# Pacing the projection products in groups of 12 and 24 in place of 5 and 8

## The chip, the core and the metric

One NeuronCore of a Trainium2 chip (trn2). The metric is device time in microseconds (us) of the whole program, which is launched once. Names of engines, as the profile gives them: PE is TensorE's matmul, PEld its weight load, DVE VectorE, ACT ScalarE, POOL GpSimd, SP the engine that issues all DMAs of this kernel. Every engine works off its own queue in a fixed order that was written down when the kernel was built; it waits where an instruction's input is not there yet, and everything behind that instruction on the same engine waits with it.

## What is computed

Two sequences of 1024 tokens (width 1024) go through the same two layers. Cut to what matters:

```python
def encoder_layer(x, c, p):
    shift, scale, gate = split(silu(c) @ w_ada + b_ada)
    h = rms_norm(x, g_pre) * (1 + scale) + shift
    proj = h @ w_in                              # the input projection
    o_a = latent_attention(...)                  # mixer a
    o_b = rwkv7(...)                             # mixer b, one scan per direction
    o_c = mamba2_ssd(...)                        # mixer c
    o_d = gated_deltanet(...)                    # mixer d, one scan per direction
    return x + gate * rms_norm(concat(o_a, o_b, o_c, o_d) @ w_out, g_post)   # the output projection
```

A pair (sequence, layer) is called a unit; there are four, run in the order (0,0), (1,0), (0,1), (1,1).

## The kernel before, in words

**Two kinds of work share TensorE.** The *bulk* is the two projections. Each fp32 operand is split into a high and a low part, and three products (high x high, high x low, low x high) stand for one fp32 product. `in_tile` makes a tile of 128 projected columns for 512 tokens: 8 slices of the contraction, three products of 128x512 each, 24 in all. Its weights come as two pairs (`halves`, high and low part of four slices), so one loaded pair feeds 12 products. `out_tiles` makes 256 output columns for 512 tokens; there a loaded pair feeds 24 products of 128x256. The whole program has 6144 products of the first kind and 3072 of the second. All of them are recorded at one line, L472, and write the tile `pj`.

The *mixers* are the rest: four heads' groups a, b, c, d with many small products, most of them 64x64, in chains that go from PE to DVE or ACT and back. Their lines that the text names: L1211, L1223, L1236, L1193 are the delta rule's scan (d); L921, L931, L944, L947, L878, L579, L891, L902 rwkv's scan (b), and L838 what prepares it; L1571 to L1573 and L1584 the attention (a); L244 the conditioning. `d` and `c` run beside each other, then `b` and `a`.

**What sets the order.** A scheduler fixes each engine's order at build time. It runs through an estimate of the program's time and takes, whenever an engine is free, the ready instruction of the highest priority. The priorities of a unit's bulk are spread over those of the mixers of the unit before (`behind`, `ahead`), so that projections of the next unit and of the last one lie between the mixers' instructions. So that the scheduler doesn't take all ready bulk at once, `paced` puts it in groups:

```python
    def paced(self, n, *mm):
        m = self.nc.tensor.matmul(*mm[:3], **mm[3]).ins
        if self.gate is not None:
            self.tc.add_manual_dep(m, self.gate[0], SYNC, reason="pace")
        if self.run == 0:
            t = self.nc.gpsimd.memset(self.token, 0.0).ins
            self.tc.add_manual_dep(t, m.name, SYNC, reason="pace")
            self.next = t.name
        self.run += 1
        if self.run == n:
            self.gate, self.run = (self.next,), 0
```

After the first product of a group, POOL sets a one-element tile, the *token* (L476). The products of the next group wait for that token. These are real semaphores: they hold on the chip as well as in the scheduler's estimate. POOL's other work is some 460 small instructions of the mixers, such as the edge memsets of rwkv's loads (L739, L741), the powers in norms (L156) and masks (L1353). The group size is `TK` for `in_tile` and `TO` for `out_tiles`. Counts of groups run on from one tile to the next.

Of the kernel before, what the change touches and what calls it, by code (L numbers as in the profile page):

```python
# [22 lines left out]
MIX = 1800  # L23
EA = 60
EB = 60
TK = 5
TO = 8
ED = 90
SB = 3
WB = 6  # L30
# [76 lines left out]
class Body:  # L107
# [204 lines left out]
    def in_tile(self, l, name, hf, hh, hl, Pd):  # L312
# [4 lines left out]
        for k in range(8):  # L317
            if k % 4 == 0:
                w2 = self.halves(("in", l, ci, k // 4), lambda: self.A["w_in"][l, ci][:, k * 128:k * 128 + 512]).rearrange("p u (k c) -> p u k c", k=4)
            for i, (a, b) in enumerate(((0, hh), (0, hl), (1, hh))):  # L320
                self.paced(TK, ps[0:M], w2[:, a, k % 4, 0:M], b[:, k, :], dict(start=(k == 0 and i == 0), stop=(k == 7 and i == 2)))
        st = self.t(pj, [128, 512], tag="st", bufs=SB)
# [26 lines left out]
    def out_tiles(self, l, ch, hh, hl, kqs, at=lambda kq: kq):  # L349
# [3 lines left out]
        for n, kq in enumerate(kqs):  # L353
            w2 = self.halves(("out", l, ch, kq), lambda: self.A["w_out"][l, ch, kq // 2][:, (kq % 2) * 512:(kq % 2) * 512 + 512]).rearrange("p u (k c) -> p u k c", k=2)
            for i in range(4):
                ps = pss[i // 2][:, i % 2]
                c = slice(i * 128, (i + 1) * 128)
                for k in range(2):
                    a, b = hh[:, at(kq) * 2 + k, c], hl[:, at(kq) * 2 + k, c]
                    first, last = n == 0 and k == 0 and i % 2 == 0, n == len(kqs) - 1 and k == 1  # L360
                    for m, (u, x) in enumerate(((a, 0), (a, 1), (b, 0))):
                        self.paced(TO, ps, u, w2[:, x, k], dict(start=first and m == 0, stop=last and m == 2, skip_group_check=True))
        return pss
# [1378 lines left out]
```

## Time and profile before

| | |
|---|---|
| median of 3 runs (lowest to highest) | 4653.71 us (4644.23 to 4672.16) |
| the profiled execution's own time | 4653.13 us |
| span from its first to its last instruction | 4651.1 us |
| PE / PEld / DVE / ACT / POOL busy | 90% / 68% / 65% / 39% / 8% of the span |
| mean granted TensorE clock | 0.895 of 2.4 GHz |

The span is 2.0 us shorter than the execution's own time, which is 0.6 us from the median. PE's busy time counts a product until its modelled end, and a product begins before the one ahead of it has ended, so two products of 0.4 us each can follow each other at 0.23 us. Rows of the trace say how long one instruction took, and in brackets how long its engine sat idle before it and what ended that.

### The profile page before, as it was taken

How to read it: one execution, taken by the hardware profiler on the slowest of the kernel's cores; microseconds unless marked ns; L12 is line 12 of the kernel's file. 1: busy time of each engine (PE TensorE's matmuls, PEld its weight loads, DVE VectorE, ACT ScalarE, POOL GpSimd, SP SyncE). 2: the span in 40 equal slices, each digit the busy share in tenths (PEclk: the TensorE clock that was granted, in tenths of full speed). 3: DMA queues.
4: the chain of work that ended last, by engine and by line, in shares of the span. 5: the costliest groups of instructions: out<-in, count | busy, mean ns of one | idle time of the engine just before them, and what ended most of it. 6: DMA issues, size and time to landing. Idle time of an engine off the chain costs nothing.

```text
span 4651.1 us, 98709 instructions
## 1 busy us (share of the span) xinstructions
PE 4177.0 (90%) x38484; PEld 3160.9 (68%) x38484; DVE 3012.1 (65%) x6237; ACT 1818.2 (39%) x4054; POOL 385.0 (8%) x2073
## 2 busy tenths in 40 slices
PE   6888998999998987989988999889897999989997
PEld 2667666667677766745767767767675776767776
DVE  2359587466559597476537959756633886865755
ACT  2433334362422433453434243335333324434433
POOL 0011001000011100000001100100001110000001
PEclk8889987989999987989989999888798999979888
DMA  5787664542676666573557767556355767665535
GB/s 205 282 268 250 236 198 152 190 145 91 203 221 228 207 190 203 151 218 134 199 194 241 256 230 215 177 182 179 123 173 183 227 225 225 209 226 151 173 114 173
DMA packets 518089, 912.85 MB, mean 196 GB/s; under 512 B 152312, under 2 KB 268536, under 8 KB 514040
## 3 DMA queue, kind: packets, MB, share of 16 engines
q1 hardware_dynamic: 517624, 906.54, 60.3%
q8 instruction: 305, 5.00, 0.4%
q14 instruction: 160, 1.31, 0.1%
HBM read 622.85 MB, written 283.43 MB: 195 GB/s over the span
## 4 chain that ended last, share of the span: by engine, by line
PE 43%; DMA 15%; DVE 13%; ACT 3%; issue 3%; SPq 1%; POOL 1%; DVEq 0%; POOLq 0%; ACTq 0%
PE pj L472 20%; PE b L838 2%; PE b L1584 1%; DVE iA L536 1%; DVE G L556 1%; SPq L145 1%; DMA G<-P 1%; PE b L1540 1%; PE b L1571 1%; PE pj L244 1%; DMA UV<-vd 1%; PE b L571 1%; DMA st<-yd 1%; DVE iT L543 1%; DMA P<-st 1%
## 5 line engine op out<-in xcount | busy, mean ns | idle before, releaser
L472 PE MATMUL pj<-hh,w 128*128 128x512 f32 (+1 forms) x4096 | 1428.5, 420 | 54.6 <-POOL token L476 27.1
L472 PEld LDWEIGHTS pj<-hh,w 128*128 128x128 f32 (+1 forms) x4096 | 785.4, 195 | 260.8 <-POOL token L476 39.8
L472 PE MATMUL pj<-hl,w 128*128 128x512 f32 (+1 forms) x2048 | 859.0, 420 | 29.8 <-POOL token L476 29.7
L472 PEld LDWEIGHTS pj<-hl,w 128*128 128x128 f32 (+1 forms) x2048 | 400.4, 195 | 130.5 <-POOL token L476 38.4
L476 POOL MEMSET token<- 1x1 f32 x1613 | 142.9, 89 | 3246.8 <-PE pj L472 3238.5
L472 PE MATMUL pj<-w,hh 128*128 128x256 f32 x1536 | 334.1, 309 | 10.2 <-ACT st L386 7.5
L472 PEld LDWEIGHTS pj<-w,hh 128*128 128x128 f32 x1536 | 263.0, 205 | 32.0 <-issue 15.5
L472 PE MATMUL pj<-w,hl 128*128 128x256 f32 x960 | 271.2, 310 | 0.0
L328 ACT COPY st<-pj 128x512 f32<-128x512 f32 (+1 forms) x192 | 112.0, 583 | 366.1 <-PE pj L472 319.4
L1575 ACT ACTIVATE pT<-b 128x512 f32<-128x512 f32 x256 | 150.2, 599 | 223.3 <-PE b L1573 219.0
L652 DVE SCALAR_TENSOR_TENSOR cva<-cvi,cw,cva 128x1024 f32<-128x1024 f32 x144 | 183.6, 1279 | 60.7 <-ACT cva L648 47.1
L1541 DVE TENSOR_REDUCE mx<-b 128x1 f32<-128x512 f32 x256 | 169.8, 685 | 57.2 <-PE b L1540 55.7
L472 PEld LDWEIGHTS pj<-w,hl 128*128 128x128 f32 x960 | 186.1, 205 | 12.9 <-issue 5.4
L342 ACT CAST w<-w 128x512 fp32r<-128x512 f32 x160 | 98.9, 619 | 244.5 <-DMA w<-w_in 163.4
L343 DVE TENSOR_TENSOR w<-w,w 128x512 fp32r<-128x512 f32 x160 | 113.2, 708 | 108.2 <-ACT w L342 102.2
L1219 ACT ACTIVATE SE<-SC,el 64x64 f32<-64x64 f32 x480 | 140.3, 338 | 80.5 <-DVE SC L1230 41.2
L1584 PEld LDWEIGHTS b<-VO,pT 128*64 128x64 f32 x4096 | 144.0, 146 | 36.6 <-issue 30.0
L938 DVE TENSOR_TENSOR ZS<-us,SE 64x128 f32<-64x128 f32 x240 | 69.1, 288 | 151.0 <-PE us L931 132.6
L1584 PE MATMUL b<-VO,pT 128*64 128x65 f32 x4096 | 162.1, 233 | 1.2 <-ACT pT L1575 1.2
L843 DVE SCALAR_TENSOR_TENSOR G<-b,Dk,mk 128x128 f32<-128x128 f32 x512 | 142.5, 343 | 27.6 <-PE b L838 26.9
L838 PE MATMUL b<-AR,BK 64*64 64x128 f32 x2048 | 151.8, 301 | 4.8 <-DVE G L843 4.6
L838 PEld LDWEIGHTS b<-AR,BK 64*64 64x64 f32 x2048 | 109.4, 145 | 51.4 <-issue 41.0
(395 smaller groups left out, 8146.7 us busy)
## 6 DMA issues: line engine op xcount, KB each, us to landing
w<-win SPq DMA_DIRECT2D x384, 512.0 KB
win<-w SPq DMA_DIRECT2D x128, 512.0 KB
P<-st SPq DMA_DIRECT2D x248, 256.0 KB
w<-wout SPq DMA_DIRECT2D x96, 512.0 KB
w<-w_in SPq DMA_DIRECT2D x128, 256.0 KB
G<-P SPq DMA_DIRECT2D x112, 256.5 KB
x<-x SPq DMA_DIRECT2D x56, 512.0 KB
cvi<-P SPq DMA_DIRECT2D x48, 512.0 KB
```

The lines of the kernel that those rows point to most:

```text
L328: nc.scalar.copy(st[0:M], ps[0:M])
L342: nc.scalar.copy(w2[:, 0], w)
L343: nc.vector.tensor_tensor(w2[:, 1], w, wf[:, 0], SUB)
L472: m = self.nc.tensor.matmul(*mm[:3], **mm[3]).ins
L476: t = self.nc.gpsimd.memset(self.token, 0.0).ins
L652: nc.vector.scalar_tensor_tensor(a, c[:, j:j + 1024], wt(j, i), a, MUL, ADD)
L838: nc.tensor.matmul(pss[x][self.half(x ^ a), i * 128:i * 128 + 128], BK[self.half(x), pr, c, a], AR[self.half(x), pr, c].rearrange("p a t - ...
L843: v.scalar_tensor_tensor(G[:, x, pr, c, :], pss[x][:, i * 128:i * 128 + 128], Dk[:, c, 2 * x + pr:2 * x + pr + 1], mk, MUL, MUL)
L1219: nc.scalar.activation(SE[half(x), pr], VS[half(x), x, pr, i, :], AF.Identity, scale=el[half(x), d, pr, c:c + 1])
L1541: v.tensor_reduce(mx[:, n, qt:qt + 1], ps, AX.X, ALU.max, negate=True)
L1575: nc.scalar.activation(pT[kt], ps, AF.Exp)
L1584: nc.tensor.matmul(po[64 * x:64 * x + 64, i, :], pT[kt][:, o:o + 64], VO[:, kt, h, :], start=(kt == 0 and i == 0), stop=(kt == 7), skip_gr ...
```

## The change

Two numbers: a group of `in_tile` has 12 products where it had 5, one of `out_tiles` 24 where it had 8.

```diff
 EA = 60
 EB = 60
-TK = 5
-TO = 8
+TK = 12
+TO = 24
 ED = 90
```

A group is now all that one loaded pair of weights feeds. The program has 640 tokens in place of 1613; no other instruction is added or removed. But the scheduler decides anew, and nearly every row of PE's order stands elsewhere. The rows below are from the orders as built; a row has the line, the operation, what it writes and reads, the size, and how many equal ones follow each other.

PE in the third unit, first scan of the delta rule, about half way. Before:

```order
L1211 MATMUL us_26898<-SC_26504,GT_26583 64x64 x4
L472 MATMUL pj_25309<-hl_25268,w_3671_25310 128x512
L472 MATMUL pj_25309<-hh_25267,w_3671_25310 128x512 x2
L472 MATMUL pj_25309<-hl_25268,w_3671_25310 128x512
L472 MATMUL pj_25309<-hh_25267,w_3671_25310 128x512
L1236 MATMUL y_26916<-SC_26504,GT_26583 64x64
L472 MATMUL pj_25309<-hh_25267,w_3671_25310 128x512
L472 MATMUL pj_25309<-hl_25268,w_3671_25310 128x512
L472 MATMUL pj_25309<-hh_25267,w_3671_25310 128x512
L472 MATMUL pj_25309<-hh_25267,w_3672_25326 128x512
L472 MATMUL pj_25309<-hl_25268,w_3672_25326 128x512
L1223 MATMUL us_26898<-SC_26504 64x64 x4
```

Of the change, at the same scan:

```order
L1211 MATMUL us_26296<-SC_25902,GT_25981 64x64 x4
L472 MATMUL pj_25236<-hh_24718,w_3727_25237 128x512
L472 MATMUL pj_25236<-hl_24719,w_3727_25237 128x512
L472 MATMUL pj_25236<-hh_24718,w_3727_25237 128x512 x2
L472 MATMUL pj_25236<-hl_24719,w_3727_25237 128x512
L472 MATMUL pj_25236<-hh_24718,w_3727_25237 128x512 x2
L472 MATMUL pj_25236<-hl_24719,w_3727_25237 128x512
L472 MATMUL pj_25236<-hh_24718,w_3727_25237 128x512 x2
L472 MATMUL pj_25236<-hl_24719,w_3727_25237 128x512
L472 MATMUL pj_25236<-hh_24718,w_3727_25237 128x512
L1236 MATMUL y_26314<-SC_25902,GT_25981 64x64
L1223 MATMUL us_26296<-SC_25902 64x64 x4
```

Two handovers of the scan had five products of bulk each; now one piece of twelve stands between L1211 and L1223. Over the whole program the bulk's 9216 products stood in 1001 unbroken runs and now stand in 766.

PE in the last unit, where rwkv's second scan ends. Before, with products of the output projection (`h`) between its steps:

```order
L472 MATMUL pj_47023<-w_6627_47024,h_6616_46916 128x256 x8
L921 MATMUL us_45012<-ZS_44825,G_43647 64x64 x4
L891 MATMUL w_44968<-G_43647,At_44964 64x64 x8
L944 MATMUL y_45028<-ZS_44825,AR_43646 64x64 x4
L947 MATMUL y_45028<-UV_44824,G_43647 64x64
L472 MATMUL pj_47023<-w_6627_47024,h_6616_46916 128x256 x4
L472 MATMUL pj_47022<-w_6628_47053,h_6616_46916 128x256 x4
L931 MATMUL us_45012<-UV_44824,bk_44871 64x64 x4
```

Of the change, four of these pairs (L921, L931) before the scan's last:

```order
L1584 MATMUL b_41089<-VO_39675,pT_41045 64x65 x5
L921 MATMUL us_44269<-ZS_44097,G_42802 64x64 x4
L1584 MATMUL b_41089<-VO_39675,pT_41045 64x65 x2
L944 MATMUL y_44285<-ZS_44097,AR_42801 64x64 x4
L1584 MATMUL b_41089<-VO_39675,pT_41045 64x65
L1584 MATMUL b_41089<-VO_39675,pT_41051 64x65 x8
L1584 MATMUL b_41089<-VO_39675,pT_41057 64x65 x2
L891 MATMUL w_44236<-G_42802,At_44232 64x64 x8
L931 MATMUL us_44269<-UV_44096,bk_44143 64x64 x4
```

Between the steps of the scan stand products of the attention; the output projection of the last unit stands behind the whole scan, 576 products in a row but for four transposes (before, 316 stood behind the scan's last product).

POOL in the last unit, where rwkv's first direction loads its inputs. Before:

```order
L739 MEMSET G_42054 128x1
L476 MEMSET token_64 1x1 x6
L739 MEMSET G_42054 128x1
L476 MEMSET token_64 1x1
L779 MEMSET G_42054 128x8
L476 MEMSET token_64 1x1 x3
L739 MEMSET G_42054 128x1
L476 MEMSET token_64 1x1 x2
L741 MEMSET G_42054 128x1 x3
L476 MEMSET token_64 1x1 x7
```

Of the change:

```order
L739 MEMSET G_41209 128x1
L779 MEMSET G_41209 128x8
L739 MEMSET G_41209 128x1 x2
L476 MEMSET token_64 1x1 x3
L739 MEMSET G_41209 128x1 x3
L476 MEMSET token_64 1x1
L741 MEMSET G_41209 128x1 x5
L779 MEMSET G_41209 128x8
L739 MEMSET G_41209 128x1
L476 MEMSET token_64 1x1
```

Over the program 232 tokens stood right behind such an instruction of the mixers; of the change, 168 do.

## Rows read from the trace of the kernel before

**Rows 1.** The page's head and its first part: busy time of each engine.

```profile
span 4651.1 us, 98709 instructions
...
PE 4177.0 (90%) x38484; PEld 3160.9 (68%) x38484; DVE 3012.1 (65%) x6237; ACT 1818.2 (39%) x4054; POOL 385.0 (8%) x2073
```

**Rows 2.** Clock of the core: span, mean granted share of TensorE's clock.

```profile
core 0: 4651.1 us, clock 0.895
```

**Rows 3.** Timeline of POOL beside an unbroken run: start, length, [idle before, what ended it].

```profile
1511.42 0.09 POOL L476 MEMSET token<- 1x1 f32 x1 [0.88 <-PE pj L472]
...
1512.55 0.09 POOL L476 MEMSET token<- 1x1 f32 x1 [1.04 <-PE pj L472]
```

**Rows 4.** Timeline of PE in the last tail: an unbroken run of 128x256 products.

```profile
4591.74 12.04 PE L472 MATMUL pj<-w,h 128*128 128x256 f32 x104
```

**Rows 5.** What line L476, the token, was, and which engine waited for it (us, times).

```profile
L476 POOL MEMSET token<- x1613: 88/88/527, 96.6 to 4628.2; 1x1 f32 x180
...
  PE pj L472: 59.2, 37
```

**Rows 6.** Timeline around the longest wait for a token.

```profile
3922.13 0.61 PE L472 MATMUL pj<-hh,w 128*128 128x512 f32 x2
...
3927.35 0.26 POOL L741 MEMSET G<- 128x1 f32 x2 [6.49 <-DMA G<-P]
...
3927.54 0.09 POOL L476 MEMSET token<- 1x1 f32 x1
...
3927.69 0.80 PE L472 MATMUL pj<-hl,w 128*128 128x512 f32 x1 [4.94 <-POOL token L476]
```

**Rows 7.** Timeline of PE in the delta rule's scan, third unit: a run of five between mixers.

```profile
2707.05 0.45 PE L1211 MATMUL us<-SC,GT 128*64 128x64 f32 x8
...
2707.43 0.50 PE L472 MATMUL pj<-hl,w 128*128 128x512 f32 x1
...
2708.79 0.68 PE L1193 MATMUL w<-GT,SC 64*64 64x64 f32 x16
...
2709.40 0.33 PE L1236 MATMUL y<-SC,GT 128*64 128x64 f32 x2
```

**Rows 8.** Stretches A:B: length, busy time (count) of PE, PEld, DVE, ACT, POOL, clock.

```profile
1714.00:1990.00 276.00, 239.77 (x2755) 193.24 (x2757) 177.50 (x380) 104.39 (x320) 22.11 (x90) 0.82 0.56 172
4040.00:4150.00 110.00, 91.70 (x1108) 80.89 (x1108) 84.14 (x201) 47.56 (x146) 12.03 (x44) 0.79 0.66 217
4230.00:4577.00 347.00, 331.44 (x3897) 270.34 (x3895) 226.18 (x471) 154.66 (x359) 17.62 (x118) 0.90 0.49 148
```

**Rows 9.** The same stretches, and one without bulk, of line L472 alone (PE, PEld).

```profile
1714.00:1990.00 276.00, 97.52 (x570) 82.67 (x570) 0.82 0.56 172
4040.00:4150.00 110.00, 42.09 (x286) 36.88 (x284) 0.79 0.66 217
4230.00:4577.00 347.00, 117.80 (x728) 102.34 (x728) 0.90 0.49 148
...
1978.00:2202.00 224.00, 0.01 (x1) 0.01 (x1) 0.86 0.55 169
```

**Rows 10.** Stretches with at most two products of bulk, all instructions, columns as in rows 8.

```profile
1978.00:2202.00 224.00, 202.35 (x1669) 110.41 (x1667) 156.93 (x331) 100.28 (x173) 6.51 (x26) 0.86 0.55 169
2990.00:3044.00 54.00, 36.75 (x506) 30.50 (x506) 34.16 (x87) 25.09 (x72) 4.42 (x7) 0.63 0.79 257
...
4108.00:4169.00 61.00, 45.41 (x574) 36.16 (x571) 35.37 (x72) 22.75 (x58) 5.68 (x6) 0.58 0.79 251
4335.00:4387.00 52.00, 48.61 (x529) 34.16 (x529) 41.95 (x96) 20.41 (x35) 1.01 (x1) 0.80 0.64 193
...
4473.00:4512.00 39.00, 33.79 (x566) 27.55 (x566) 16.48 (x46) 19.77 (x54) 0.17 (x1) 0.94 0.42 131
```

**Rows 11.** Stretches rich in bulk, all instructions, columns as in rows 8.

```profile
1300.00:1700.00 400.00, 358.95 (x2802) 281.84 (x2800) 296.35 (x569) 143.56 (x286) 41.33 (x247) 0.94 0.70 228
...
3700.00:3950.00 250.00, 231.20 (x1895) 175.62 (x1892) 182.82 (x348) 80.85 (x186) 28.64 (x161) 0.97 0.68 220
```

## The prediction, made blind

> **What bounds the kernel now.** I read the page's first part before anything else [rows 1, 2]: PE is busy 4177.0 of 4651.1 us, so it sits idle for 474 us, a tenth of the span; DVE (65%) and ACT (39%) have room, and POOL, at 8%, has plenty. Work on PE is the same before and after, since no product is added or taken away. The time can therefore change in three ways only: PE's idle time shrinks or grows, the clock moves, or switching between kinds of product costs more or less. The granted clock is 0.895 of 2.4 GHz on average, and not even: stretches that are rich in bulk have 0.94 and 0.97 [rows 11], stretches with next to none have 0.58 to 0.86, but for one with 0.94 [rows 10].
>
> Next come the prices of a bulk product. Within an unbroken run of 128x512 products the tokens follow each other every 1.13 us [rows 3], one per group of five: 0.227 us a product. A run of 104 products of 128x256 takes 12.04 us [rows 4]: 0.116 us each. All bulk together is 6144 x 0.227 + 3072 x 0.116 = 1751 us; the other 2900 us of the span are mixers, with bulk put into their waits. Two views then say what the groups do. The waits of the token [rows 5] show how much PE loses to pacing itself, 59.2 us in 37 waits. And stretches with and without bulk [rows 8 to 11] show what a mixer costs when bulk stands in its waits and when it stands alone. That is what a coarser group trades away.
>
> **The change, part by part.** *973 tokens fewer.* A token is a POOL memset of 88 ns [rows 5], 86 us less of POOL's work in all. POOL has 92% room, so this is worth nothing in itself. It would count only if POOL were the one waited for, and that is the next term.
>
> *Waits for a token* (A). The longest shows the pattern [rows 6]: POOL stood 6.49 us before a memset of rwkv's load, because a transfer had not landed; the token was behind that memset in POOL's queue, and PE waited 4.94 us for it with bulk, and with every mixer product queued behind that bulk. A token is set after a group's first product. The rest of the group runs meanwhile, so POOL may be late by 4 x 0.227 = 0.9 us before PE stands; of the change, by 11 x 0.227 = 2.5 us, 1.6 us more. Taking 1.6 us off each of the 37 waits one by one leaves 21.5 us. Only 168 tokens, not 232, stand right behind such an instruction now, so the rest is 21.5 x 168/232 = 15.6 us. Gain: 59.2 − 15.6 = 44 us. Bounds: nothing, if each wait taken away is met by another right behind it (the mixer waits for the same transfer), and 59, if all go. I take 44, since the arithmetic of each wait supports it.
>
> *Fewer switches* (B). A run of five between mixer products begins at 2707.43 and the next mixer product at 2708.79 [rows 7]: 1.36 us, where five products in steady pace take 1.13. The two edges cost 0.21 us. Where the bulk leaves, an edge between two mixer products stays, for which I put half of that. So a run that is merged with another saves 0.1 us, and there are 235 runs fewer (1001 to 766): 24 us. Bounds: 0 and 235 x 0.21 = 49.
>
> *Stretches without bulk* (C). This is the cost. A group of twelve is one block of 2.7 us where five were 1.1, and the scheduler puts it where it finds room and leaves long stretches with none. Three places which held bulk now hold next to none: the mixers of 1714 to 1990 (570 products of 128x256, now none), of 4040 to 4150 (286, now some 29), and rwkv's end at 4230 to 4577 (728, now some 52). The bulk is not lost; it goes elsewhere (next term). The question is how quickly the mixers of these stretches run without it. With it, taking the bulk's own steady time out of the stretch [rows 8, 9], they run at (276 − 66)/2185 = 96 ns, (110 − 33)/822 = 94 ns and (347 − 84)/3169 = 83 ns a mixer product: bulk beside them, waits included.
>
> What they take alone no row tells of these very mixers, so I take bounds from stretches that are bare already [rows 10]. Two chains take 106.5 ns a product (54 us/506 and 61/574) at clocks of 0.63 and 0.58; a stretch of scan filled with attention takes 69 ns (39/566) at 0.94, one in between 98 ns (52/529), the conditioning's neighbour 134 (224/1669); all five together 430/3844 = 112 ns. The first two stretches are chains, and I put them at 106.5 ns: 2185 x 10.5 ns = 23 us and 822 x 12.5 ns = 10 us. The third is now filled with attention, which stands between the steps of the scan as the order shows; I put it at 91 ns, midway from its 83 now to the 98 of the nearest filled row: 3169 x 8 ns = 25 us. Sum +59, with rounding. Bounds: 0, if attention and conditioning fill as in the 69 ns row, and 142 (35 + 15 + 92) at 112 ns throughout.
>
> The clock goes with it. The chain rows show what a mixer alone gets: PE idles a quarter to a third of the time there, and the granted clock lies near the lower level, 1.2 GHz. The Trainium skill, TensorE: Matmul & The Clock Gate, section "A second HAM failure mode: psum-queue depth-cycling", states that small idle gaps of PE between groups of products send the clock back and forth, so that throughput suffers between bursts. The rows agree at 0.58 and 0.63. But the bare row of 4473 with its idle of 13% still has 0.94 [rows 10]. If the rule held for the attention-filled stretch too, it would take the chains' 106.5 ns and cost 3169 x 23.5 ns = 74 us in place of 25; the sum would end at 4673 us rather than at the forecast.
>
> *The bulk that was moved* (D). Some 174 us of it (66 + 30 + 78) stand elsewhere now, mostly ahead, in stretches that hold bulk already; there is then more to put into each wait. Where bulk is rich, PE still idles 60 of 650 us, 9.2% [rows 11]. The rest of the span, without the three stretches and the bare ones, has 3630 us and, of the 474 us of idle, about 360. Its bulk grows from 1568 to 1742 us, 11%. In proportion that fills 40 us of idle time, and I halve it, since a block of 2.7 us overfills a wait of one or two: 20 us. Bounds: 0, and 88 if the rest came to the 7.5% of the densest row (3700 to 3950).
>
> *Transfers and the other engines.* The count of DMAs, and of DVE's and ACT's instructions, is unchanged. Weights are loaded with the bulk that needs them, and now sometimes earlier in a burst; the DMA engines are not what a steady run waits for [rows 3], so I put this at nothing. If they were, it would show as PE waiting for `w`, a few us per burst.
>
> *Sum.* −44 − 24 + 59 − 20 = −29 us. From the profiled execution's 4653.1 us that gives **4624 us**; the median of the runs shown is 0.6 us higher, so nothing is added for that.
>
> **The rivals.** *The bare stretches cost nothing* (faster). Attention and conditioning are as good a filler as bulk; the 69 ns row speaks for it, and the order, which puts attention between the steps. Against it speak both chain rows. C falls away: −88 us, 4565 us.
>
> *The bare stretches are paid in full* (slower). They run at the pooled 112 ns with the clock of the chains, and the moved bulk fills nothing where it lands, because a block of twelve makes a chain wait for what it saves. −44 − 24 + 142 = +74 us, 4727 us. For it: four of the five bare rows lie above what the same kind of mixer takes with bulk. Against it: the last unit's stretch is full of attention. It turns slower than before where C passes 68 us with D at nothing, and slower by more than 0.5% from 91 us, which is 3169 products at 101 ns with the other two as above. The skill's rule, above, speaks for this side, though its own sum stays within 0.5%.
>
> *The change does nothing that can be measured.* The token's wait stands where a transfer is late, and the mixer behind waits for the same transfer: A shrinks to a few us, and B and C cancel. 4653 us. For it: the wait at 3922 to 3927 is one of a DMA [rows 6]. Against it: bulk could run through that wait, as no transfer of its own was missing.
>
> **How the numbers follow.** About 0.5%, 23 us, is what a measurement of this kernel can tell from no change: 4630 to 4677 us. The forecast has 0.42, with its own range of 4590 to 4650, and some three fifths of it (0.26) is faster by over 0.5%. The first rival has 0.16, all faster; the second 0.28, all slower; no effect has 0.14. Faster is 0.26 + 0.16 = 0.42, the same 0.16 + 0.14 = 0.30, slower 0.28; as the edges of 'no effect' are soft, 0.03 of it goes over to the two sides, 0.01 and 0.02: 0.43, 0.27 and 0.30. The two ends of the bounds together are 4653 − 44 − 24 − 88 = 4497 and 4653 + 142 = 4795, both with several extremes at once. The range reaches to the first rival and just past the second, 4560 to 4735 us, which leaves out one in ten on each side.
>
> **What would show it.** A is right if the waits of PE for the token come to 10 to 20 us. B: a run of twelve between mixers takes about 12 x 0.227 + 0.21 = 2.9 us. C: the mixers of the three stretches, found by their lines, take 100 to 110 ns (first two) and 85 to 98 ns a product, with a clock of about 0.6 and 0.85. D: the rich stretches of the first and last unit's start have less than 9.2% of idle. The forecast is wrong if PE's idle time grows by over 50 us, or if the mean clock falls by more than 0.02: then the bare stretches decide. It is wrong the other way if rwkv's end, with attention alone, runs as quickly as with bulk.

## The result: slower by 1.3%, with fewer waits for the token and more for everything else

The change took 4711.28 us in the median of 4 runs, the kernel before 4661.23 us in 4 runs on the same chip. The ratio is 1.013, with a 95% interval of 1.0097 to 1.0163: slower, clearly. The profiled execution of the change took 4723.94 us (span 4722.2), 71 us more than that of before [rows 1]; it is the slowest of the four (4697.85 to 4723.94), so some 20 of the 71 us are chance. The page's head and first part, and the core's clock:

```profile
span 4722.2 us, 97792 instructions
...
PE 4127.7 (87%) x38484; PEld 3173.2 (67%) x38484; DVE 3004.9 (64%) x6237; ACT 1819.7 (39%) x4054; POOL 307.1 (7%) x1100
```

```profile
core 0: 4722.2 us, clock 0.882
```

PE's busy time fell by 49 us and its idle time rose from 474 to 594.5 us, by 120 (busy time is modelled to each product's end, so the two are exact only as a sum). The token's line, and who waited for it:

```profile
L476 POOL MEMSET token<- x640: 88/88/401, 95.5 to 4696.3; 1x1 f32 x160
...
  PE pj L472: 9.7, 9
...
  PE yd L1363: 5.4, 3
```

The bulk waited 59.2 us for tokens [rows 5] and now waits 9.7; 5.4 more are put down to mixer c's products at L1363. So the part of the change that was aimed at the pacing worked. Other waits grew by some 165 us.

Where, a split by units shows. I cut both programs at the first product of mixer c (L1318) of units 2, 3 and 4; the mixers ahead of the last cut and behind it are then equally many in both (6806 behind it). First before, then the change, all instructions (columns as in rows 8):

```profile
0.00:1418.50 1418.50, 1263.71 (x10509) 924.10 (x10510) 847.62 (x1752) 538.74 (x1109) 123.12 (x659) 0.90 0.62 204
1418.50:2515.60 1097.10, 974.05 (x9210) 716.73 (x9209) 718.03 (x1525) 444.68 (x1002) 86.21 (x439) 0.88 0.60 193
2515.60:3646.50 1130.90, 1029.11 (x9553) 789.52 (x9552) 744.44 (x1528) 450.98 (x1008) 96.87 (x524) 0.89 0.62 197
3646.50:4651.10 1004.60, 910.10 (x9217) 730.51 (x9215) 702.03 (x1435) 383.81 (x937) 78.76 (x451) 0.90 0.60 188
```

```profile
0.00:1457.40 1457.40, 1272.62 (x10601) 938.72 (x10602) 823.98 (x1730) 541.93 (x1117) 101.70 (x379) 0.91 0.62 207
1457.40:2630.80 1173.40, 1042.09 (x9707) 788.37 (x9705) 786.72 (x1604) 473.98 (x1048) 75.80 (x263) 0.88 0.63 202
2630.80:3720.60 1089.80, 967.93 (x9297) 760.67 (x9298) 701.75 (x1475) 428.66 (x969) 74.22 (x267) 0.89 0.59 186
3720.60:4722.20 1001.60, 845.03 (x8883) 685.41 (x8881) 692.40 (x1431) 375.12 (x923) 55.37 (x191) 0.84 0.54 171
```

And line L472 alone in the last unit, before and after:

```profile
3646.50:4651.10 1004.60, 474.33 (x2411) 371.95 (x2410) 0.90 0.60 188
```

```profile
3720.60:4722.20 1001.60, 359.03 (x2077) 305.48 (x2076) 0.84 0.54 171
```

The last unit has 1536 products of 128x256 in both; the rest are of 128x512. At the steady prices of rows 3 and 4 its bulk is 376.6 us before and 300.8 after. So the last unit takes as long as it did (1001.6 against 1004.6 us) with 76 us less to do: a mixer product takes (1004.6 − 376.6)/6806 = 92.3 ns before and 103.0 after, and the granted clock is 0.84, not 0.90. The first three units take 74 us longer (3720.6 against 3646.5) and do 76 us more bulk; there the change is even, to 2 us. (Two other executions of the very same order there, early12 and after_dbl below, came out 26 us better and 4 us worse than even: read one execution's units to some 25 us.) **Net of the bulk at its steady price, all of the loss appears in the last unit.** It is the unit that has no next one whose bulk could fill its waits. PE's idle time by itself grew in both parts, by 58 us in the first three units and by 62 in the last, so the first three, where 46 of the 59.2 us of token waits stood, are no quicker for having lost them.

One wait there is long. PE in the change:

```profile
4045.41 3.88 PE L838 MATMUL b<-AR,BK 64*64 64x128 f32 x32 [0.39 <-DVE G L843]
4079.06 1.20 PE L472 MATMUL pj<-w,hh 128*128 128x256 f32 x4 [29.77 <-issue]
4081.34 0.58 PE L472 MATMUL pj<-w,hl 128*128 128x256 f32 x1 [1.08 <-DVE hl L377]
```

SP, DVE and ACT at that place:

```profile
4074.37 0.38 SPq L145 DMA_DIRECT2D x<-o  x1
```

```profile
4072.01 0.75 DVE L410 SCALAR_TENSOR_TENSOR st<-st,ors,st 128x512 f32<-128x512 f32 x1
4073.21 0.69 DVE L411 TENSOR_TENSOR st<-st,x 128x512 f32<-128x512 f32 x1
```

```profile
4077.91 1.04 ACT L376 CAST hh<-x 128x1024 fp32r<-128x1024 f32 x1 [42.23 <-DMA x<-o]
```

The profile names no releaser ("issue"), but the rows around it do: this is the third unit's output projection, second half. Its input is loaded into `x`, a ring of two buffers that the first half's finishing (L410, L411) uses too. The load goes out at 4074.37, behind most of that finishing, ACT copies at 4077.91, and PE goes on at 4079.06. The load is not later than it was: it goes out 40 us behind the first half's last product, in the kernel before 48 us. Nor is the first half quicker: it takes 94 us in 27 unbroken runs, before 88 us in 31. What differs is the order between the two halves (all instructions, before and in the change):

```profile
4107.10:4168.90 61.80, 45.52 (x576) 36.31 (x576) 36.13 (x73) 23.61 (x61) 5.68 (x6) 0.59 0.78 247
```

```profile
4034.20:4079.10 44.90, 13.13 (x162) 11.01 (x161) 41.50 (x110) 2.43 (x7) 2.13 (x3) 0.58 0.52 170
```

Some 575 mixer products cover the load before, some 160 in the change. Before, no wait of over 5 us stands in the last unit.

The three stretches that lost their bulk, found again by the position of their mixers in PE's order, and the two that were rich (columns as in rows 8; of the fourth and fifth row 1141 and 710 products are bulk, of the second 29, of the others none):

```profile
1804.70:2049.10 244.40, 196.98 (x2152) 121.83 (x2154) 166.47 (x394) 93.26 (x263) 14.76 (x17) 0.75 0.56 180
4153.70:4235.80 82.10, 64.35 (x860) 53.89 (x859) 49.08 (x128) 38.12 (x122) 4.71 (x6) 0.65 0.54 169
4298.00:4613.70 315.70, 273.80 (x3166) 193.04 (x3166) 211.86 (x451) 135.06 (x279) 9.74 (x27) 0.80 0.30 84
1395.50:1783.70 388.20, 333.90 (x2921) 281.83 (x2918) 302.70 (x542) 157.38 (x344) 37.26 (x118) 0.87 0.72 231
3769.80:4003.60 233.80, 223.17 (x1974) 180.29 (x1969) 173.29 (x307) 97.28 (x229) 21.69 (x84) 0.96 0.70 223
```

Bare, they take 113.6, 94.7 and 99.7 ns a mixer product; with bulk they had taken 96, 94 and 83.

### The profile page after: what moved, and what is told of

Same layout as the page of the kernel before. It is cut to its first block, busy times and chain, and to the rows that moved or that the text cites. A ratio compares the mean times of both kernels' runs of the same rounds, so it can differ in the third digit from the quotient of the medians.

```text
span 4722.2 us, 97792 instructions
## 1 busy us (share of the span) xinstructions
PE 4127.7 (87%) x38484; PEld 3173.2 (67%) x38484; DVE 3004.9 (64%) x6237; ACT 1819.7 (39%) x4054; POOL 307.1 (7%) x1100
## 5 line engine op out<-in xcount | busy, mean ns | idle before, releaser
L472 PE MATMUL pj<-hh,w 128*128 128x512 f32 (+1 forms) x4096 | 1413.0, 414 | 45.8 <-ACT w L342 13.9
L472 PEld LDWEIGHTS pj<-hh,w 128*128 128x128 f32 (+1 forms) x4096 | 790.6, 194 | 256.6 <-issue 65.2
L472 PE MATMUL pj<-hl,w 128*128 128x512 f32 (+1 forms) x2048 | 835.8, 409 | 0.0
L472 PEld LDWEIGHTS pj<-hl,w 128*128 128x128 f32 (+1 forms) x2048 | 399.2, 195 | 93.6 <-issue 13.0
L472 PE MATMUL pj<-w,hh 128*128 128x256 f32 x1536 | 326.8, 309 | 40.7 <-issue 32.6
L472 PEld LDWEIGHTS pj<-w,hh 128*128 128x128 f32 x1536 | 263.5, 209 | 56.0 <-issue 44.4
L472 PE MATMUL pj<-w,hl 128*128 128x256 f32 x960 | 261.3, 305 | 9.3 <-DVE hl L377 6.9
L476 POOL MEMSET token<- 1x1 f32 x640 | 57.1, 89 | 2685.8 <-PE pj L472 2673.4
L472 PEld LDWEIGHTS pj<-w,hl 128*128 128x128 f32 x960 | 184.6, 207 | 15.7 <-DVE hl L377 9.3
L1584 PEld LDWEIGHTS b<-VO,pT 128*64 128x64 f32 x4096 | 142.1, 142 | 20.5 <-issue 16.7
```

Of the source, the lines that this page charges most:

```text
L1584: nc.tensor.matmul(po[64 * x:64 * x + 64, i, :], pT[kt][:, o:o + 64], VO[:, kt, h, :], start=(kt == 0 and i == 0), stop=(kt == 7), skip_gr ...
```

## Experiments

Each ratio below is to the kernel before, run on the same chip in the same turn. Theory 1 says that the bulk is spent ahead, and the last unit lacks filler. Theory 2 says that a chain has to wait behind a block of 12 or 24, wherever it stands. The last unit of each profiled execution, cut as above; bulk is priced as in rows 3 and 4, and 6670 to 6814 mixer products stand behind the cut:

| run | ratio (95%) | groups, last unit | its bulk, us | its length, us | ns a mixer product |
|---|---|---|---|---|---|
| before | 1 | 5, 8 | 376.6 | 1004.6 | 92.3 |
| the change | 1.013 (1.0097 to 1.0163) | 12, 24 | 300.8 | 1001.6 | 103.0 |
| k12_o8 | 1.0204 (1.0178 to 1.023) | 12, 8 | 257.4 | 961.4 | 105.5 |
| k5_o24 | 1.0151 (1.0104 to 1.0199) | 5, 24 | 383.6 | 1083.9 | 102.9 |
| deep2 | 1.0134 (1.0106 to 1.0163) | 5, 8 | 306.5 | 1021.1 | 105.9 |
| tok_last | 1.0154 (1.0127 to 1.018) | 12, 24 | 331.0 | 1022.8 | 103.7 |
| early12 | 1.0144 (1.0112 to 1.0176) | 5, 8 | 300.8 | 1005.0 | 103.5 |
| late12 | 1.0131 (1.0097 to 1.0164) | 12, 24 | 376.6 | 1065.2 | 101.2 |
| late12_ed | 1.0079 (1.0054 to 1.0105) | 12, 24 | 376.6 | 1042.2 | 97.8 |
| g6_12 | 1.0147 (1.0115 to 1.0179) | 6, 12 | 385.4 | 1052.8 | 97.9 |
| ctl_eb50 | 1.0046 (1.0022 to 1.007) | 5, 8 | 376.6 | 1020.4 | 94.6 |
| after_load | 1.0073 (1.0053 to 1.0094) | 12, 24 | 283.3 | 988.6 | 105.8 |
| before_load | 1.0097 (1.0066 to 1.0127) | 5, 8 | 377.5 | 1038.9 | 97.3 |
| sw2 | 1.0151 (1.013 to 1.0173) | 5, 8 | 347.6 | 1023.6 | 101.2 |
| swa2 | 1.0089 (1.0068 to 1.0109) | 5, 8 | 383.4 | 1039.4 | 96.4 |
| after_dbl | 1.0145 (1.0116 to 1.0174) | 12, 24 | 389.8 | 1003.8 | 90.2 |
| before_dbl | 1.0231 (1.0205 to 1.0258) | 5, 8 | 465.7 | 1110.1 | 94.7 |
| g4_6 | 1.0275 (1.0242 to 1.0308) | 4, 6 | 378.9 | 1054.0 | 100.0 |
| early12_load | 1.0072 (1.0045 to 1.01) | 5, 8 | 283.3 | 997.5 | 107.1 |
| swa3_load | 0.9998 (0.9977 to 1.002) | 5, 8 | 319.6 | 990.0 | 98.5 |

**Which of the two numbers.** One of them changed at a time:

```diff
-TK = 5
+TK = 12
 TO = 8
```

> Groups of 12 for the input projection, 8 (as before) for the output projection. In the order as built, 1494 us worth of bulk (at 0.227 and 0.116 us a product) stands ahead of the last unit's mixer c, where the kernel before has 1374 and the change 1450; so the last unit has 119 us less to fill its waits with. Theory 1 (the bulk runs ahead and the last unit is left without filler): as slow as the change or slower, 4700 to 4740 us, the loss again in the last unit, whose mixers take over 100 ns a product. Theory 2 (a block of 12 or 24 makes chains wait behind it, wherever it stands): about half of the loss, 4680 to 4695 us, spread over the units. If the output projection's 24 is the cause: 4650 to 4670 us.

```diff
 TK = 5
-TO = 8
+TO = 24
```

> Groups of 5 as before for the input projection, 24 for the output projection. In the order, 1368 us worth of bulk stands ahead of the last unit's mixer c (before 1374). Theory 1 (running ahead): as before or a little better, 4630 to 4670 us, last unit's mixers at about 92 ns a product as before. Theory 2 (block size): about half of the loss, 4680 to 4695 us.

Both are slower than before, so neither half of the change is the harmless one. k12_o8 came out as theory 1 had it in sign, but slower still, and some 45 us of its loss lie ahead of the last unit's cut; that wasn't expected. k5_o24 goes against theory 1: its last unit has all its bulk (383.6 us), and takes 79 us more. By its trace two waits of 15.9 and 10.1 us stand behind rwkv's last scan; for the other 50 us or so I found no such place. It is also the run whose times spread most, 4722 to 4798 us.

**Small blocks, loose brake; large blocks, tight brake.** In deep2 a group waits for the token of the group before the last:

```diff
...
-            self.gate, self.run = (self.next,), 0
+            self.gate, self.older, self.run = self.older, (self.next,), 0
```

> Groups of 5 and 8 as before, but a group waits for the token of the group before the last one, so up to two groups are let through. Blocks stay small, the brake is loosened: in the order, 1445 us worth of bulk stands ahead of the last unit's mixer c (before 1374, the change 1450). Theory 1 (running ahead): slower as the change is, 4690 to 4720 us, with the loss in the last unit. Theory 2 (block size): not slower, 4620 to 4665 us, since the token's waits get shorter and the blocks don't grow.

deep2 is as slow as the change, with blocks of 5 and 8. Its last unit looks like that of the change, too: 306.5 us of bulk and 105.9 ns a mixer product. So blocks of 12 and 24 aren't needed for the loss. The blocks didn't stay as they were, though: two groups can follow each other, and the bulk stands in 892 unbroken runs, between the 1001 of before and the 766 of the change. That bulk may run ahead is the likelier reading of this run, and not the only one. tok_last keeps the blocks and sets the token late:

```diff
-        if self.run == 0:
+        if self.run == n - 1:
```

> Groups of 12 and 24 as in the change, but the token is set after the last product of a group, not the first: every group is followed by a pause. In the order, 1420 us worth of bulk stands ahead of the last unit's mixer c, midway between before (1374) and the change (1450). Theory 1 (running ahead): midway, 4670 to 4695 us, less what PE waits for tokens, which can be read from the trace. Theory 2 (block size): as slow as the change or slower, 4705 us and above.

It missed theory 1's range: 1.0154. PE waited 79.4 us for tokens in 157 waits, 20 us more than before, and the first unit alone took 1470 us against 1418, with 16 us more bulk. The pause costs by itself, so this run can't tell the theories apart.

**Where in the program.** `TK` and `TO` are switched when the output projections beside and behind the last unit begin. This is early12, which begins with 12 and 24; late12 begins with 5 and 8 and has 12 and 24 here:

```diff
...
+            TK, TO = 5, 8
             mix(3, 16, lambda: run_out(2), lambda: out_last([(1, (3, 2), True, False)]), start=EC / 100)
```

> Groups of 12 and 24 for all bulk recorded up to the last unit's own input projection, then 5 and 8 for the output projections that run beside and after the last unit's mixers. In the order, 1450 us worth of bulk stands ahead of the last unit's mixer c, as in the change. Theory 1 (bulk spent ahead, last unit without filler): as slow as the change, ratio 1.010 to 1.018. Theory 2, now narrowed to the last unit's own blocks of 24 (the only place where a late chain can't be made up): as before, ratio 0.995 to 1.004.

> The reverse: groups of 5 and 8 up to the last unit's own input projection, then 12 and 24. In the order, 1374 us worth of bulk stands ahead of the last unit's mixer c, the same as before, and the first three units are unchanged. Theory 1: as before, ratio 0.997 to 1.005. Theory 2, narrowed: as slow as the change or as the run with 5 and 24, ratio 1.010 to 1.018, with the loss in rwkv's second scan of the last unit.

early12 decides for theory 1 as far as it goes: with blocks of 5 and 8 in the last unit, that unit is as slow as the change's, to half a nanosecond a product. It has the wait between the halves too, of 40.2 us, with groups of 8, so the wait doesn't come from blocks of 24:

```profile
4056.96 1.55 PE L472 MATMUL pj<-w,hh 128*128 128x256 f32 x4 [40.21 <-issue]
```

But late12 was as slow, with the first three units as before to 4 us (cut at 3650.6) and all the bulk left for the last. So either suffices, and the two don't add up. Its trace shows one wait of PE that before doesn't have:

```profile
4651.17 3.10 PE L472 MATMUL pj<-w,h 128*128 128x256 f32 x24 [1.68 <-DVE hh L450]
4657.88 1.09 PE L610 MATMUL w<-c_ident,Y 128*128 128x128 f32 x4 [3.62 <-DVE Y L692]
4679.81 5.37 PE L472 MATMUL pj<-w,h 128*128 128x256 f32 x22 [20.84 <-ACT h L438]
```

The last piece of the output projection waits until rwkv's last output is normalised, stored, loaded and split. The bulk behind the scan covers the wait, as far as it doesn't need that output: 39 us stand there before, 21 in late12, and in either the last 96 products (11 us) need it. g6_12 and ctl_eb50 were run beside them:

```diff
-TK = 5
-TO = 8
+TK = 6
+TO = 12
```

> Groups of 6 and 12, a small step. In the order, 1366 us worth of bulk stands ahead of the last unit's mixer c (before 1374). Theory 1: as before, ratio 0.995 to 1.005. Theory 2: a fifth of the way to the change, 1.002 to 1.006. If any new order is as slow as the change, a ratio of 1.01 and more.

```diff
-EB = 60
+EB = 50
...
-EC = 60
+EC = 50
```

> Groups of 5 and 8 as before; only the priorities of the bulk of units 1 to 3 are spread over the first 50% of the mixers in place of 60%. A control: the bulk ahead of the last unit's mixer c is 1374 us worth, as before, the brake is the same, but the order differs in many places. Theories 1 and 2 both expect about no change, ratio 0.995 to 1.005. If any new order is as slow as the change, a ratio of 1.01 and more.

A step to 6 and 12 costs as much as the whole change, which neither theory had; it meets the mark that was set for "any new order is as slow", 1.01. It has 24 us behind the scan and waits 23.3 us there. The control says what a new order alone may cost at the same brake: 0.5%, against 1.3 to 1.5% of the three others.

**The two long waits.** In after_load and before_load the second half's loads are written ahead of the first half's finishing:

```diff
...
+        for hf in range(2):
+            ssq = self.t(sp, [128, 4, 4], tag="ssq", bufs=2)
+            hh, hl = load(hf)
+            if done is not None:
+                finish(*done)
+            for ch in range(4):
...
+            done = hf, ssq
+        finish(*done)
```

(`load` and `finish` hold the lines that stood there; `ssq` gets a second buffer.)

> The change, with one thing moved: in the output projection of the first three units, the loads of the second half's inputs are written ahead of the finishing of the first half (norm, residual, store), whose tiles come from the same ring of two buffers. In the change's trace PE stands 29.8 us at 4049 in the last unit, before the first product of the second half of the projection that runs there; its loads had waited behind that finishing. Theory 3 (a large piece of the loss is this one wait, which opens because the first half is done in one burst): the wait goes, the time falls by 20 to 30 us against the change, ratio to before 1.003 to 1.008. Theory 1 (chains without filler, whatever stands at one place): the wait turns up elsewhere, ratio 1.010 to 1.016.

> The same move in the kernel before, as a control. There no wait of over 5 us stands at that place. Both theories: no change, ratio 0.997 to 1.004. In the order, only 20 us worth of bulk stands behind rwkv's last scan product (before 39); if those 39 are what covers the wait for the last mixer's output, as the runs late12 (20.8 us) and g6_12 (23.3 us) suggest, a wait of 15 to 22 us opens there and the ratio is 1.003 to 1.005.

Theory 3 (a large piece of the loss is this one wait) holds in size: 1.013 to 1.0073 is 27 us, give or take some 18 by the two intervals, and the longest wait of PE in the last unit of after_load is 11.0 us. It doesn't hold in place. The last unit of after_load, all instructions:

```profile
3707.50:4696.10 988.60, 822.54 (x8669) 668.59 (x8667) 675.52 (x1414) 367.97 (x919) 52.04 (x182) 0.83 0.54 166
```

PE is idle for 166 us there, with the long wait gone, and for 157 in the change; from early12 to early12_load, which loses a wait of 40.2 us, it stays at 162. In the last unit other waits took its place, as theory 1 had it, with 105.8 ns a mixer product and still less bulk. What was gained stands ahead of the cut (3707.5 against 3720.6 us, and 3678.8 against early12's 3696.2, each with some 18 us more bulk and 136 more mixer products), where the same loads of the second and third unit were moved. The control hit the other mechanism: with 20 us behind the scan a wait of 21.6 us opened there, as expected, though the ratio of 1.0097 shows some 20 us more. late12_ed then put the cover back into late12, by priorities alone:

```diff
...
-            self.behind(p0 + int((p1 - p0) * start), p0 + (p1 - p0) * ED // 100, n, fs)
+            self.behind(p0 + int((p1 - p0) * start), p0 + (p1 - p0) * (115 if u == 3 else ED) // 100, n, fs)
```

> The run late12 (12 and 24 in the last unit alone) with the priorities of the last unit's bulk spread to 115% of its mixers in place of 90%, so that 34 us worth of bulk, not 21, stand behind rwkv's last scan product. If what stands there covers the wait for the last mixer's output (20.8 us in late12): that wait shrinks to 5 us or less and the ratio falls from 1.013 to about 1.009 to 1.010. If the blocks of 24 are the cause by themselves: unchanged, 1.012 and more.

PE's waits of late12 and of late12_ed in the last unit:

```profile
PE pj L472 <- ACT h L438: 20.8, 1, 20.8
```

```profile
PE pj L472 <- ACT h L438: 4.0, 1, 4.0
```

From 1.0131 to 1.0079, or 24 us, which the two intervals leave open by some 20; the wait became 17 us shorter. So the cover behind the scan is worth about what the wait says. The 0.8% that is left has blocks of 24 and all the bulk; what makes it isn't settled.

**Filler given back.** Is the last unit of the change short of filler, or bound by chains? Every product of the third unit's output projection is done twice:

```diff
...
-                    for m, (u, x) in enumerate(((a, 0), (a, 1), (b, 0))):
+                    for m, (u, x) in enumerate(((a, 0), (a, 1), (b, 0)) * times):
```

> The change, with every product of the third unit's output projection done twice (this doubles a sum that is normalised afterwards, and changes the output a little). That is 768 products, 89 us at 0.116 us, all of them beside the last unit's mixers, with no transfer more. If the last unit lacks filler (theory 1), most of the 89 us go into waits that are there anyway: 25 to 50 us more than the change, ratio to before 1.018 to 1.024. If its waits are those of chains behind blocks, which more blocks make no shorter (theory 2): 75 to 95 us more, ratio 1.029 to 1.034.

> The same doubling in the kernel before, whose last unit has 376 us worth of bulk already. Theory 1: little idle time is left to fill, 60 to 85 us more, ratio 1.013 to 1.018. If the last unit is bound by chains in either kernel: 30 to 50 us more, ratio 1.006 to 1.011.

This is the clearest of the runs. The last unit of after_dbl and of before_dbl, all instructions:

```profile
3726.90:4730.70 1003.80, 897.92 (x9651) 754.54 (x9649) 693.12 (x1431) 374.08 (x923) 58.12 (x225) 0.90 0.56 171
```

```profile
3673.10:4783.20 1110.10, 1011.65 (x9985) 822.15 (x9983) 703.75 (x1435) 382.99 (x937) 85.44 (x547) 0.92 0.55 171
```

89 us of additional products cost the change nothing that can be told: its last unit takes 1003.8 us instead of 1001.6, and the ratio goes from 1.013 to 1.0145. In the kernel before the same products cost 2.3%, some 108 us. With the filler, the clock of the change's last unit is back at 0.90, and the coarse groups are the faster: 4732.42 us against 4773.82. That filler was missing is shown: with 389.8 us of bulk the change's last unit takes as long as that of before with 376.6 (1003.8 against 1004.6 us), in blocks of 24 and with the change's order of mixers, so neither of the two makes it slow once it is filled. Of the additional and the moved products 633 stand among the mixers of rwkv's end, which take 87 ns there instead of 99.7, and the wait of 29.8 us is gone: the longest of that unit is 6.0. Both theories had expected more of the price to stay in after_dbl, and less of it in before_dbl, which paid more than the 89 us.

**Giving it back without additional work.** The groups are made small again earlier, so that the lead is used up before the last unit (sw2 from the third unit's mixers on, swa2 from its late input projection on):

> Groups of 12 and 24 only for bulk recorded up to unit 2's input projections (the first two units' mixers and the beginning of the third), then 5 and 8. In the order, 1404 us worth of bulk stands ahead of the last unit's mixer c (before 1374, the change 1450) and 42 us behind the last scan product (before 39). Theory 1: what the bulk was ahead is spent down in the third unit, the last unit is nearly as before; the gain in tokens and switches of two units stays: ratio 0.995 to 1.003. If blocks of 12 and 24 cost wherever they stand (theory 2): half of the loss, ratio 1.006 to 1.008.

> Groups of 12 and 24 only for bulk recorded up to the second unit's mixers, 5 and 8 from the late part of the third unit's input projection on. In the order, 1368 us worth of bulk stands ahead of the last unit's mixer c (before 1374) and 38 us behind the last scan product (before 39). Theory 1: as before or a little faster, ratio 0.993 to 1.000. Theory 2: a third of the loss, ratio 1.004 to 1.006.

Theory 1's numbers failed. The shortage moved: the third unit has 372 and 364 us of bulk in place of 446, and takes, net of its bulk, 19 and 39 us more than before. In these two runs the lead, where it was run down, starved the unit that it was run down in. swa2 shows something else, too: its last unit has all its bulk and still takes 35 us longer than before. A step in the other direction:

```diff
-TK = 5
-TO = 8
+TK = 4
+TO = 6
```

> A step in the other direction: groups of 4 and 6. In the order, 1372 us worth of bulk stands ahead of the last unit's mixer c (before 1374) and 39 us behind the last scan product (before 39). Theory 1 and 2: the last unit as before or better, but more switches (1134 unbroken runs against 1001) and less cover for a late token; net about no change, ratio 0.996 to 1.004. If any new order loses: 1.005 and more.

1.0275: the slowest of all, and it lost most in the third unit (1205.8 us against 1130.9, with 9 us less bulk). I have no cause for it. Last, the loads moved as in after_load, together with groups of 5 and 8 from the last unit's output projections on (early12_load) or one step earlier (swa3_load):

> Groups of 12 and 24 until the last unit's own input projection is recorded, 5 and 8 after it, with the second half's loads moved ahead as in after_load. In the order, 1468 us worth of bulk stands ahead of the last unit's mixer c and 60 us behind the last scan product. Theory 1 (the last unit lacks filler, whatever the size of its groups): as after_load, ratio 1.004 to 1.010. Theory 2 (blocks of 24 in the last unit): better than after_load by 20 us and more, ratio 1.003 or less.

> The same, but groups of 5 and 8 begin one step earlier, with the late part of the last unit's input projection, so that less of it is done ahead: 1432 us worth of bulk ahead of the last unit's mixer c in place of 1468. Theory 1: half of the distance to before is made up, ratio 1.000 to 1.006, the best of the kernels with coarse groups. If the order itself decides, anything from 1.00 to 1.015.

early12_load equals after_load, so the size of the groups in a starved last unit hardly matters. swa3_load, which leaves the last unit 36 us more bulk, is the best of the coarse ones and equals the kernel before (0.9998). No version beat it. Eight of the other orders leave the last unit its bulk (376.6 to 385.4 us: k5_o24, late12, late12_ed, g6_12, ctl_eb50, before_load, swa2, g4_6), and in each it takes 16 to 79 us longer than in the kernel before. So missing filler isn't the only way to lose time here, and that nearly any other order loses some is a rival that these runs leave standing for those versions; for the change's own last unit after_dbl speaks against it.

## Why the prediction was wrong

The forecast was 4624 us and faster; it became slower, by 50 us in the median, close to the second rival (4727 us), which had 0.28. That rival met the number by luck: it had 142 us for C and nothing for D, where 92 and a loss of 72 were measured.

- **A, the token's waits: right.** 15.6 us were to be left, 9.7 are (15.1 with the mixer's), a gain of 44 to 50 as against 44.
- **B, the switches: the single edge right, the sum open between the forecast and its upper bound.** A run of twelve in the change's third unit (2771.02 to 2773.97, first and last rows below) takes 2.95 us, where 12 x 0.227 is 2.72; the forecast said 2.9. Its edges cost 0.23 us, as those of five did [rows 7], so 235 runs fewer are worth up to 235 x 0.21 = 49 us. PE's busy time fell by just that, 49 us, where 24 were forecast; but busy time moves with the clock and the waits, too (L472's alone fell by 93 us, from 2171.3 to 2078.4), so this is no proof of 49.

```profile
2770.64 0.45 PE L1211 MATMUL us<-SC,GT 128*64 128x64 f32 x8
2771.02 0.50 PE L472 MATMUL pj<-hh,w 128*128 128x512 f32 x1
...
2773.65 0.39 PE L472 MATMUL pj<-hh,w 128*128 128x512 f32 x1
2773.97 0.33 PE L1236 MATMUL y<-SC,GT 128*64 128x64 f32 x2
```

- **C, the bare stretches: right in kind, too small.** Predicted were 106.5, 106.5 and 91 ns; measured 113.6, 94.7 and 99.7, each outside the range that was given for it (100 to 110 for two, 85 to 98 for the third). With the predicted counts this is 2185 x 17.6 + 822 x 0.7 + 3169 x 16.7 = 92 us instead of 59. Midway between 83 and 98 was the wrong choice for the attention-filled stretch: it lies just above the upper row, and its clock fell to 0.80.
- **D, the moved bulk: the step that failed.** It was to fill 20 us of idle time where it lands. In the first three units 76 us more bulk made the program 74 us longer, in spite of what A and B gave there, so nothing of any filling can be seen. Of the rich stretches one became better (idle 4.5% of 3769.8 to 4003.6, 7.5% before) and one worse (14% of 1395.5 to 1783.7, 10% before) [rows 11]. What A, B at its upper bound and C leave of the 71 us is 71 + 44 + 49 − 92 = 72 us lost, where 20 were to be won; with B at its forecast it is 47. These are not the 73 us that the last unit lost net of its bulk: 54 of those are C's second and third stretch, which stand in that unit.
- **What the sum lacked.** It took the moved bulk for a gain where it lands, and priced its absence in three stretches alone. Bulk done ahead at full price pays only if the unit that gives it up gets shorter, and the last unit doesn't: 1001.6 us with 300.8 us of bulk, 1004.6 with 376.6. The prediction had both facts on the table, 576 products behind the scan and a lead of the bulk, and drew no price from them. after_dbl and before_dbl show that price: 89 us of products for nothing in the one, 108 us in the other. How the 72 us divide among the units is not measured.
- **Transfers** were put at nothing, and one wait was a transfer's: 29.8 us behind a shared ring of two buffers. The prediction did name PE waiting for bulk inputs as the sign, but for the weights, not for `x`. What that wait cost is open: moving the loads won 27 us in after_load, but not in the last unit.
- **The clock** was given as a companion of C. It fell where filler was short (0.84 in the last unit) and came back with it (0.90 in after_dbl). Of the two signs that the forecast named against itself, PE's idle time passed its mark (120 us more, 50 allowed), and the mean clock didn't (0.895 to 0.882, 0.02 allowed). The Trainium skill, TensorE: Matmul & The Clock Gate, section "A second HAM failure mode: psum-queue depth-cycling", had been weighed as speaking for a dearer attention-filled stretch; the stretch's 0.80 at 13% idle agrees in direction, where the row of 4473 had 0.94 at the same idle.
- **The third rival** (no effect) is excluded by the interval.

Left open: why blocks of 24 cost 0.8% in a last unit that has its bulk and its cover (late12_ed), why 4 and 6 are so slow, what eats the gain of A and B in the first three units, and how much of any of it is the particular order: the control's 0.5% is one draw.

## What to carry to other kernels

Filler that was spent early was missed at the end here; when a change lets low-priority work run ahead, price the stretch that has nothing behind it, usually the last one. A brake on such work (here the token's short groups) may be worth more than the waits that it causes: 50 us of them went, and the kernel became slower. To find out whether a stretch lacks filler or is bound by its chain, double some independent work in it: what costs nothing fits into its waits. And a long wait that is closed isn't time won: look whether the engine's idle time in that stretch falls with it.

## What was unexpected

- 768 products of 128x256, 89 us at the steady price, took 2.2 us in the change's last unit (1001.6 to 1003.8 us).
- The wait for the last mixer's output opened in each run that had 24 us of bulk or less behind the last scan: one wait of 20.8, 21.6 and 23.3 us with 21, 20 and 24 us behind it, two of 15.9 and 10.1 us with 11; with 31 us (ctl_eb50) it was 5.3, with 34 (late12_ed) 4.0.
- Groups of 6 and 12 were as slow as 12 and 24, and 4 and 6 slower than either. The time isn't a smooth function of the group's size.
